# Sliding windows by DMA: thirteen staged batches instead of twelve, 32 KB packets on both queues, and a last store in three parts

## The chip, the core and the metric

The kernel runs on one core of one Trainium2 chip. The time is the device time of one execution, in microseconds; a smaller one is better. The program uses no compute engine. It consists of DMAs, which SP (SyncE) and ACT (ScalarE) issue, each on a queue of its own, and which the core's 16 DMA engines carry out. A DMA is cut into packets, and each engine works on the packets of both queues. A semaphore counts the engines that have finished a DMA: it rises by 16 for a whole one, and SP and ACT can wait for its value.

## The reference

The input is a float32 array of 32 batches, 4096 rows and 256 columns. Windows of 64 rows are taken every 32 rows, 127 in each batch, and written out one after the other:

```python
n_windows = (length - window_size) // stride + 1
result = np.zeros((batch, n_windows, window_size, dim), dtype=np.float32)
for i in range(n_windows):
    start = i * stride
    result[:, i] = x[:, start:start + window_size].copy()
```

A batch is 128 blocks of 32 rows, 32 KB each. Window w is blocks w and w + 1, 64 KB. Every block but the first and the last of a batch is thus written twice: as the first half of window w and as the second half of window w - 1. The output has 266.3 MB, the input 134.2 MB.

## The kernel before, in words

There are two ways to make a batch.

*Copied batches* go from HBM to HBM, issued by SP (`copy`, line 93). For a group of windows one DMA reads 64 KB for each window, at steps of 32 KB, and writes 64 KB for each. A copied batch is 8.3 MB through the DMA engines; HBM reads 8.3 MB and writes 8.3 MB. Before, a batch is three DMAs (`COPY_PARTS`, line 16): 80 windows in packets of 16 KB, 32 windows in packets of 32 KB, 15 windows in packets of 16 KB.

*Staged batches* go through on-chip memory, issued by ACT. `load` (line 75) brings the 128 blocks into a tile, one block of 32 KB per partition, 4.2 MB. `store` (line 83) writes the tile out twice: once with block p as the first half of window p, once with block p as the second half of window p - 1. That is 4.2 + 8.4 = 12.6 MB through the engines, but HBM reads only 4.2 MB. Before, the packets are 16 KB (`BLOCK_PARTS`, line 14). There are five tiles; the load of batch n waits for the stores of batch n - 5. ACT issues load 0 and load 1, and then in turn: wait for load n, two stores of n, load n + 2.

The stores of a staged batch have no gaps, and so each writes one half window too many: block 127 has no window 127, and lands in the first half window of the next batch; block 0 has no window -1, and lands in the last half window of the batch before. These *stray rows* must be overwritten. For most neighbours the order does it: the copy of a neighbour is issued by SP only after the staged batch has been stored (`after_store`, lines 134 to 137). These copies are called tied. Four neighbours, `EARLY`, are copied first of all, under a semaphore of their own; the staged batches beside them are stored only after that (line 146), and what they spoil is copied once more at the end by a *mend* of 32 KB, 16 packets of 2 KB (`half`, line 46; lines 151 to 158). Of the staged batches, numbered from n = 0, the last ones need mends.

Staged are the odd batches 1 to 23, twelve of them; copied are the other twenty. `_order` (line 102) lists the copies: the four early ones, then the untied ones, with each tied one inserted at a place that grows with the number of the last staged batch it waits for. SP issues all copies in this order, then waits for the early ones, issues the seven mends as their stores finish, waits for everything, and clears twelve semaphores one at a time (lines 159 to 163). The two queues are independent but for those semaphores, and they share the 16 engines.

Of the kernel before, what the change touches and what calls it, by code (L numbers as in the profile page):

```python
# [1 line left out]

# [4 lines left out]


STAGED = tuple(range(1, 24, 2))
BUFS = 5  # L10

EARLY = (18, 20, 22, 24)

BLOCK_PARTS = 2

COPY_PARTS = ((80, 4), (32, 2), (15, 4))


class _Geometry:


    def __init__(self, x, out, W, S):
        self.B, self.L, self.D = x.shape
        self.x, self.out = x, out
        self.n_win = (self.L - W) // S + 1
        self.n_blk = self.L // S
        self.blk = S * self.D
        self.win = W * self.D
        assert W == 2 * S and self.n_blk == self.n_win + 1 == 128

    def src(self, b, block, dims):

        at = (b * self.n_blk + block) * self.blk
        return bass.AP(self.x.tensor, self.x.offset + at, dims)

    def dst(self, b, half, dims):

        at = b * self.n_win * self.win + half * self.blk
        return bass.AP(self.out.tensor, self.out.offset + at, dims)

    def rows(self, b, w0, n):

        s, d = [[self.blk, n], [1, self.win]], [[self.win, n], [1, self.win]]
        return self.dst(b, 2 * w0, d), self.src(b, w0, s)

    def half(self, b, half, block):

        dims = [[self.blk // 16, 16], [1, self.blk // 16]]
        return self.dst(b, half, dims), self.src(b, block, dims)


class _Kernel:
    def __init__(self, nc, g, tiles):
        self.nc, self.g, self.tiles = nc, g, tiles
        self.loaded = [nc.alloc_semaphore(f"loaded{i}") for i in range(len(tiles))]
        self.stored = [nc.alloc_semaphore(f"stored{i}") for i in range(len(tiles))]
        self.copied = nc.alloc_semaphore("copied")
        self.early = nc.alloc_semaphore("early")
        self.count = {}

    def start(self, engine, out, in_, sem, parts=1):
        engine.dma_start(out=out, in_=in_, max_dma_last_dim=65536 // parts).then_inc(sem, 16)
        self.count[id(sem)] = self.count.get(id(sem), 0) + 16

    def all_of(self, engine, sem):
        engine.wait_ge(sem, self.count[id(sem)])

    def slot(self, n):
        return divmod(n, len(self.tiles))

    def after_store(self, engine, n):
        turn, i = self.slot(n)
        engine.wait_ge(self.stored[i], 32 * (turn + 1))

    def load(self, n):

        g, (_, i) = self.g, self.slot(n)
        if n >= len(self.tiles):
            self.after_store(self.nc.scalar, n - len(self.tiles))
        src = g.src(STAGED[n], 0, [[g.blk, g.n_blk], [1, g.blk]])  # L80
        self.start(self.nc.scalar, self.tiles[i][:, :], src, self.loaded[i], 2 * BLOCK_PARTS)

    def store(self, n):

        g, (turn, i) = self.g, self.slot(n)
        self.nc.scalar.wait_ge(self.loaded[i], 16 * (turn + 1))
        for half in (0, -1):
            dst = g.dst(STAGED[n], half, [[g.win, g.n_blk], [1, g.blk]])  # L90
            self.start(self.nc.scalar, dst, self.tiles[i][:, :], self.stored[i], 2 * BLOCK_PARTS)

    def copy(self, b, sem):

        w = 0
        for rows, parts in COPY_PARTS:
            self.start(self.nc.sync, *self.g.rows(b, w, rows), sem, parts)
            w += rows
        assert w == self.g.n_win


def _order(B):


    near = {b for s in STAGED for b in (s - 1, s + 1)}
    order = list(EARLY) + [b for b in range(B) if b not in near and b not in STAGED]
    tied = sorted(near - set(EARLY))
    n = len(order) + len(tied)
    for b in tied:
        behind = max(STAGED.index(s) for s in (b - 1, b + 1) if s in STAGED)  # L110
        order.insert(-(-(2 * behind + 5) * n // (2 * len(STAGED))), b)
    return order


@with_exitstack
def kernel(
    ctx: ExitStack,
    tc: tile.TileContext,
    x: bass.AP,
    window_size: bass.AP,  # L120
    stride: bass.AP,
    out: bass.AP,
):
    nc = tc.nc
    W, S = int(window_size), int(stride)
    g = _Geometry(x, out, W, S)
    assert 0 not in STAGED and g.B - 1 not in STAGED
    pool = ctx.enter_context(tc.tile_pool(name="blocks", bufs=1))
    tiles = [pool.tile([g.n_blk, g.blk], x.dtype, name=f"xb{i}") for i in range(BUFS)]

    with tc.tile_critical():
        k = _Kernel(nc, g, tiles)
        for b in _order(g.B):
            if b not in EARLY:
                for s in (b - 1, b + 1):
                    if s in STAGED:
                        k.after_store(nc.sync, STAGED.index(s))
            k.copy(b, k.early if b in EARLY else k.copied)
        k.load(0)
        waited = False  # L140
        last = len(STAGED) - 1
        for n, s in enumerate(STAGED):
            if n < last:
                k.load(n + 1)
            if not waited and (s - 1 in EARLY or s + 1 in EARLY):
                k.all_of(nc.scalar, k.early)
                waited = True
            k.store(n)


        k.all_of(nc.sync, k.early)
        for n, s in enumerate(STAGED):
            if s - 1 in EARLY or s + 1 in EARLY:
                k.after_store(nc.sync, n)
            if s - 1 in EARLY:
                k.start(nc.sync, *g.half(s - 1, 2 * g.n_win - 1, g.n_blk - 1), k.copied)
            if s + 1 in EARLY:
                k.start(nc.sync, *g.half(s + 1, 0, 0), k.copied)
        for n in range(len(STAGED)):
            k.after_store(nc.sync, n)  # L160
        k.all_of(nc.sync, k.copied)
        for sem in [*k.loaded, *k.stored, k.copied, k.early]:
            nc.sync.sem_clear(sem)


# [1 line left out]
_INS = ['x', 'window_size', 'stride']  # L167
_OUTS = [((32, 127, 64, 256), 'float32')]

_NUMBERS = {'window_size': 64, 'stride': 32}  # L170


# [26 lines left out]
```

## Time and profile before

| | us |
|---|---|
| median of three runs | 767.76 (767.14 to 767.97) |
| the profiled execution | 768.4 |
| its span, first to last instruction | 766.6 |
| mean rate of the DMA engines over the span | 414 GB/s |
| read from and written to HBM | 217.02 and 267.35 MB |

The page names two queues: q1 is SP's, q10 is ACT's. "DMA share" in a list of stretches is the mean share of time that the 16 engines spent on packets; records of neighbouring packets overlap slightly, so 1.01 can occur. The rate counts each byte once, also for a copy that reads and writes HBM. A line "SPq ... <- DMA ..." in the list of waits says how long SP waited in total for DMAs of that kind, how often, and the longest wait. The trace also has a record of every packet: queue, size, start and duration, without the engine.

The DMAs of the profiled execution, by kind, with the median time from issue to landing:

| DMA | number | KB each | us to landing |
|---|---|---|---|
| copy of 80 windows, SP | 20 | 5120 | 114.8 |
| copy of 32 windows, SP | 20 | 2048 | 116.7 |
| copy of 15 windows, SP | 20 | 960 | 97.7 |
| mend, SP | 7 | 32 | 48.3 |
| load, ACT | 12 | 4096 | 123.2 |
| store, ACT | 24 | 4096 | 84.6 |

### The profile page before, as it was taken

What the parts mean: (1) busy time and instruction counts of PE and PEld (TensorE: products, weight loads), DVE (VectorE), ACT (ScalarE), POOL (GpSimd) and SP (SyncE); (2) the same over time, 40 slices, a digit from 0 to 9 for tenths busy, and PEclk for the clock granted to TensorE, in tenths of its full rate; (3) what the DMA queues carried; (4) which work ended last, traced back from release to release, by engine and by line L of the source; (5) the groups of instructions that cost most, each with busy time, mean ns of one, the idle gap of its engine ahead of it and who ended that gap; (6) DMA issues with size and microseconds to landing.
All of it is one profiled execution on the core that took longest, in us unless ns stands there. A gap on an engine that the chain in (4) does not pass through costs nothing. (4 is left out here: it accounts for less than half of the span.)

```text
span 766.6 us, 180 instructions
## 1 busy us (share of the span) xinstructions
POOL 0.2 (0%) x4
## 2 busy tenths in 40 slices
POOL 0000000000000000000000000000000000000000
DMA  8999999999999999999999999999999999999996
GB/s 371 425 410 421 405 428 431 408 411 427 423 415 421 431 415 425 432 408 416 427 420 417 431 420 420 423 428 410 414 427 419 422 428 418 417 428 421 420 406 237
DMA packets 19837, 317.70 MB, mean 414 GB/s; under 512 B 1628, under 2 KB 1628, under 8 KB 1740
## 3 DMA queue, kind: packets, MB, share of 16 engines
q1 hardware_dynamic: 10044, 166.70, 51.9%
q10 hardware_dynamic: 9792, 151.00, 47.3%
q14 instruction: 1, 0.01, 0.0%
HBM read 217.02 MB, written 267.35 MB: 632 GB/s over the span
## 5 line engine op out<-in xcount | busy, mean ns | idle before, releaser
L180 POOL MEMSET const-bfloat16-1.0<- 128x1 bf16 x1 | 0.1, 102 | 0.0
L180 POOL MEMSET const-uint8-127<- 128x1 uint8 x1 | 0.1, 102 | 0.0
L180 POOL MEMSET const-float32-0.0<- 128x1 f32 x1 | 0.1, 99 | 0.2 <-issue 0.2
L180 POOL MEMSET const-float32-1.0<- 128x1 f32 x1 | 0.1, 99 | 0.0
## 6 DMA issues: line engine op xcount, KB each, us to landing
out_dram<-in_x_dram SPq DMA_DIRECT2D x20, 5120.0 KB, 114.8
out_dram<-xb ACTq DMA_DIRECT2D x24, 4096.0 KB, 84.6
xb<-in_x_dram ACTq DMA_DIRECT2D x12, 4096.0 KB, 123.2
out_dram<-in_x_dram SPq DMA_DIRECT2D x20, 2048.0 KB, 116.7
out_dram<-in_x_dram SPq DMA_DIRECT2D x20, 960.0 KB, 97.7
out_dram<-in_x_dram SPq DMA_DIRECT2D x7, 32.0 KB, 48.3
```

Source lines behind the costliest of these rows:

```text
L180: nc = _bacc.Bacc("TRN2", target_bir_lowering=False, num_devices=1)
```

## The change

- The staged batches are 1, 3, ... 25, thirteen, and nineteen are copied. The early ones are 20, 22, 24 and 26.
- Every large packet is 32 KB, on both queues (`start` has `parts=2` as its default, 65536 / 2).
- A copied batch is two DMAs instead of three: 112 windows (seven for each engine) and 15 windows.
- The last staged batch (25) is stored in three parts of its partitions, each with its two halves: 0 to 31, 96 to 127, then 32 to 95. The first two contain block 0 and block 127, and so all stray rows; their four DMAs count on a new semaphore, `fringe`. The last two mends wait for `fringe`; the mends of earlier staged batches wait for their stores as before.
- At the end SP waits for every semaphore, those of the loads too, and clears them all with one instruction over a range.

The order on ACT is otherwise the same: load n + 2 after the stores of n, five tiles. ACT's wait for the early copies stands ahead of the stores of n = 9 (batch 19), before it was n = 8 (batch 17).

```diff
-STAGED = tuple(range(1, 24, 2))
+STAGED = tuple(range(1, 26, 2))
-EARLY = (18, 20, 22, 24)
-BLOCK_PARTS = 2
-COPY_PARTS = ((80, 4), (32, 2), (15, 4))
+EARLY = (20, 22, 24, 26)
+EVEN = 112
+LAST = ((0, 32), (96, 32), (32, 64))
...
-    def start(self, engine, out, in_, sem, parts=1):
+    def start(self, engine, out, in_, sem, parts=2):
         engine.dma_start(out=out, in_=in_, max_dma_last_dim=65536 // parts).then_inc(sem, 16)
...
-        self.start(self.nc.scalar, self.tiles[i][:, :], src, self.loaded[i], 2 * BLOCK_PARTS)
+        self.start(self.nc.scalar, self.tiles[i][:, :], src, self.loaded[i])
...
-    def store(self, n):
+    def store(self, n, p0, rows, sem=None):
...
         for half in (0, -1):
-            dst = g.dst(STAGED[n], half, [[g.win, g.n_blk], [1, g.blk]])
-            self.start(self.nc.scalar, dst, self.tiles[i][:, :], self.stored[i], 2 * BLOCK_PARTS)
+            dst = g.dst(STAGED[n], 2 * p0 + half, [[g.win, rows], [1, g.blk]])
+            self.start(self.nc.scalar, dst, self.tiles[i][p0 : p0 + rows, :], sem or self.stored[i])
...
-        for rows, parts in COPY_PARTS:
-            self.start(self.nc.sync, *self.g.rows(b, w, rows), sem, parts)
-            w += rows
...
+        k.copy(b, 0, EVEN, k.early if early else k.copied)
+        k.copy(b, EVEN, n_win - EVEN, k.early if early else k.copied)
...
+        k.after_load(nc.scalar, n)
+        if n < last:
+            k.store(n, 0, g.n_blk)
+        else:
+            for p0, rows in LAST:
+                alone = p0 > 0 and p0 + rows < g.n_blk
+                k.store(n, p0, rows, None if alone else k.fringe)
...
+        if n == len(STAGED) - 1:
+            k.all_of(nc.sync, k.fringe)
+        elif s - 1 in EARLY or s + 1 in EARLY:
+            k.after_store(nc.sync, n)
...
-        for sem in [*k.loaded, *k.stored, k.copied, k.early]:
-            nc.sync.sem_clear(sem)
+def _end(k):
+    for sem in k.sems:
+        k.all_of(k.nc.sync, sem)
+    used = sorted(sem.num for sem in k.sems)
...
+    k.nc.sync.sem_clear(range(used[0], used[-1] + 1))
```

## The prediction

> **What bounds the kernel now.** I read the page's slices first, then its queue part, then stretches of the trace, then the waits, and last the packet records (queue, size, start, duration).
>
> ```profile
> span 766.6 us, 180 instructions
> DMA  8999999999999999999999999999999999999996
> DMA packets 19837, 317.70 MB, mean 414 GB/s; under 512 B 1628, under 2 KB 1628, under 8 KB 1740
> ...
> q1 hardware_dynamic: 10044, 166.70, 51.9%
> q10 hardware_dynamic: 9792, 151.00, 47.3%
> ...
> HBM read 217.02 MB, written 267.35 MB: 632 GB/s over the span
> ```
>
> No compute engine does anything; the 16 DMA engines are busy in every slice but the last. q1 is SP's queue (20 copied batches), q10 is ACT's (12 staged batches). Their shares add to 99.2% of 766.6, 760.5 us per engine. So every packet counts, and the time is the number of packets on an engine times the time of one, plus a start and an end.
>
> ```profile
> core 0: us, POOL busy (x), PEclk, DMA share, GB/s
> 6.00:26.00 20.00, 0.00 (x0) 1.00 1.01 432
> 657.00:670.00 13.00, 0.00 (x0) 1.00 1.00 408
> 720.00:748.00 28.00, 0.00 (x0) 1.00 0.94 403
> 752.00:756.00 4.00, 0.00 (x0) 1.00 0.92 348
> 756.00:758.00 2.00, 0.00 (x0) 1.00 0.78 286
> 758.00:760.00 2.00, 0.00 (x0) 1.00 0.74 246
> 760.00:762.00 2.00, 0.00 (x0) 1.00 0.29 110
> 762.00:764.00 2.00, 0.00 (x0) 1.00 0.06 22
> ```
>
> The last column is the rate. Clean stretches run at 432 GB/s, others lose some 5% with the engines still busy: there single packets take longer. From 720 the share is 0.94, as one engine of 16 has run out: the 15-row copies use 15 engines, so one has less to do. After 753 only copies are left (the last record of q10 ends at 753.4), and 15 engines move 348 instead of 403. That stretch and the engines' unequal ends, 758 to 764, are the tail.
>
> ```profile
> SPq L62 <- DMA out_dram<-xb: 61.2, 2, 40.2
> SPq L73 <- DMA out_dram<-xb: 19.2, 3, 9.4
> SPq L66 <- DMA out_dram<-in_x_dram: 7.7, 1, 7.7
> ```
>
> SP's waits for stores before mends and in the final list cost nothing while q1 holds queued copies. Only the last, 7.7 us for `copied`, sets the end: the last landing releases it at 764.9, twelve semaphore clears run from 764.9 to 765.6, and the closing barrier ends at 766.6.
>
> From the packet records: a 16 KB packet takes 611 ns undisturbed, a 32 KB one 1211. They overlap by a few ns; the next one on an engine starts 607.1 and 1209.4 ns after (432 GB/s over 16 engines also gives 607). Time over 611 and 1211, between 6 and 748 us: 16 KB of q1 1.87%, 32 KB of q1 3.16%, 16 KB of q10 2.70%; with start and tail 18.8 us per engine.
>
> **The account of before, for one of the 15 full engines.** A copied batch gives it 20 packets of 16 KB (80 rows), 4 of 32 KB (32 rows) and 4 of 16 KB (15 rows); a staged one 16 for the load and 32 for the two stores. In all 20 x 24 + 12 x 48 = 1056 of 16 KB and 80 of 32 KB: 1056 x 0.6071 + 80 x 1.2094 = 737.9 us. Plus 2.0 to the first packet, 18.8 of slow packets, and some 1.8 of mends and completion packets: 760.5, the mean end. The last engine ends 3.3 later, 763.8, its landing is seen at 764.9, the end at 766.6. The profiled execution took 768.4, 1.8 outside its span, and lies 0.6 above the median of 767.76; I add differences to the median.
>
> **The change, part by part.**
> *One more staged batch, and 32 KB packets.* A copied batch is now 16 packets of 32 KB on a full engine, a staged one 24: 19 x 16 + 13 x 24 = 616, times 1.2094 is 745.0 us. Against 737.9 that is **+7.1**: 8 packets more (+9.7), and 528 pairs of 16 KB packets turned into one each, 4.8 ns saved per pair (-2.5). The engines are never idle, so nothing hides it.
>
> *Slow packets.* No row has 32 KB on both queues. Slow packets go with copies: while the 80-row copies ran (equal packets on both queues) q1 lost 1.85% and q10 1.95%; while the 32-row copies ran (32 KB beside 16 KB, q1 taking 58% of engine time) they lost 3.0% and 5.65%. A copy reads and writes HBM, a staged packet does one of the two, so the larger share of copies asks more of HBM; alone the copies made 348 GB/s, 696 read and written. After the change packets are equal throughout. For q1 I take 1.85% of 304 x 1.2094 = 367.7: 6.8 us. For q10 the nearest is its whole run, as its loads and second stores lose most whatever copy lies beside them: 2.70% of 377.3, 10.2. With 0.6 at the start 17.6: **-1.2**. Ends: 0.96% (stretches of 4 us with a q1 share of 47 to 53%) gives 7.2 us, -11.6; 3.9%, the mean beside the 32-row copies, gives 29.1, +10.3.
>
> *The tail.* q1 has 304 packets to send, q10 312; with the queues alternating and q1 starting 3.8 us late (first packet at 5.8, against 2.0; three packets) q10 ends last with some 5 packets, 6 us of stores without copies. So the copies-only stretch goes (2.72 MB between 752 and 764 at 403 would be 6.7 us; it took until 763.8), but unequal ends, grown over the whole run, stay. Ends: 0 and -3.3; I take **-1.0**, nearer to 0, as equal rates in the tail do not level engines that arrive 5 us apart.
>
> *Fringe first.* The last batch's stores go out as partitions 0-31, 96-127, then 32-95: six DMAs for two, the same packets. Each of the four added costs ACT some 0.4 to 0.5 us of issue (median store 442 ns), covered by queued packets; at an empty queue it would be 2 us. SP's two last mends wait for the fringe instead of the whole store, with 8 packets per engine (9.7 us) still to come behind it. A mend issued at 756.2 had landed by 764.9 in a crowded queue, so they end about when the middle does: 0, and +3 if the middle is through first. Each fringe DMA has two partitions per engine; the nearest rows are ordinary stores: at their 2.7%, 0.3 us on 8 packets, inside the 10.2. Ends: 0, and +10 if each of the 8 takes twice as long (the slowest q10 packet took 1766 ns, 2.9 times 611).
>
> [...]
>
> *The end.* One ranged clear replaces twelve, of 57 ns each: **-0.6**. The longer list of waits passes at once but for its last few entries, 65 ns each (+0.1).
>
> *The order on SP and ACT.* EARLY moves by two, the wait for `early` from the store of n = 8 to n = 9; those copies land by 160 us, hundreds earlier. Tied copies wait for stores on SP. At 216 GB/s for each queue (half of 432) a copied batch takes 38.5 us and a staged one 58.3. The tightest is batch 18, the eighteenth copied, due on the engines at 5.8 + 17 x 38.5 = 660; the store it waits for (n = 9, after ten loads and stores and one load more) lands near 2 + 16.8 MB / 216 GB/s + 9 x 58.3 = 605. So SP's queue does not run dry: 0. SP issues 38 copies rather than 60, each behind a full queue: 0. If a wait did starve q1, q10 would keep the engines busy and the copies would trail alone, at 348 instead of 403: 1.3 us for each 10 us of lag.
>
> Sum: 7.1 - 1.2 - 1.0 + 0 - 0.6 + 0.1 = **+4.4** on 767.76: 772.2. I say **772**.
>
> **The rivals.**
> *Faster: equal packets empty the waits for HBM.* For it: beside equal shares 4 us stretches lost only 0.96%, and HBM bytes fall from 484 to 480 MB while DMA bytes rise. Against it: part of the slow packets are q10's own at the turn from store to load, and their count rises. Price: 2.0 + 745.0 + 7.2 + 1.6 + about 2.5 to the last engine, 1.0 + 1.2 to the end: 760.5, a time of 761.6. It decides below 13 us of slow packets. Chance 0.34.
>
> *Slower still: the fringe or 32 KB packets are expensive.* 3.9% slow, or a fringe at double time: +10 on the sum, 778 to 784. For it: 32 KB packets lost 3.16%, the most of any kind. Against: the 16 KB ones beside them lost 5.65%. Chance 0.16.
>
> *The tail does not do what it says:* q1 loses six turns, its copies end last, and the mends wait behind them: tail saving gone, +1 to +3: 773 to 775. Chance 0.08.
>
> **How the numbers follow.** My forecast, 768 to 776, has 0.42. Less than 0.2% (1.5 us) is no change to this measurement. Faster takes the first rival, 0.34; same the lower edge of the forecast, 0.10; slower the rest, 0.56. The range goes from 760, the faster case, to 780, inside the expensive one, leaving 0.2 out.
>
> **What the profile will show.** 321.8 MB, 158.4 of it on q1 and 163.6 on q10; 1209 ns between undisturbed 32 KB packets. Slow packets near 17 us: 7 or 29 picks a rival. The 0.94 share some 45 us from the end; q10 the last queue with data, at 420 GB/s or more after q1 is dry; fringe packets no slower than other stores; a single clear. I am wrong if slow packets do not follow the share of copies, if the fringe doubles, or if q1 ends last.

## The result

| | before | changed |
|---|---|---|
| median of seven runs, us | 767.51 (765.99 to 769.03) | 773.32 (771.89 to 779.07) |
| ratio | | 1.0092, 95% interval 1.0074 to 1.0110 |

The changed kernel is 0.9% slower, 5.8 us, where the prediction said 4.4 and 772. Five of its seven executions lie between 771.9 and 773.5; the other two took 777.1 and 779.1. The profiled execution is the one of 779.1, and its trace shows something that is not in the sum: one engine that came late. Its page:

```profile
span 776.9 us, 155 instructions
...
DMA  9999999999999999999999999999999999999993
...
DMA packets 11319, 321.95 MB, mean 414 GB/s; under 512 B 1389, under 2 KB 1389, under 8 KB 1501
...
q10 hardware_dynamic: 5680, 163.58, 50.0%
q1 hardware_dynamic: 5639, 158.37, 48.3%
HBM read 212.89 MB, written 267.42 MB: 618 GB/s over the span
```

The mean rate, 414 GB/s, is that of before; there are 4.25 MB more to move, though HBM has 4.1 MB less to read and write. The stretches at the end, in the columns busy share and GB/s:

```profile
core 0: us, POOL busy (x), PEclk, DMA share, GB/s
6.00:700.00 694.00, 0.00 (x0) 1.00 1.00 424
738.00:750.00 12.00, 0.00 (x0) 1.00 0.93 394
752.00:756.00 4.00, 0.00 (x0) 1.00 0.92 343
756.00:760.00 4.00, 0.00 (x0) 1.00 0.96 400
760.00:764.00 4.00, 0.00 (x0) 1.00 0.67 271
764.00:768.00 4.00, 0.00 (x0) 1.00 0.23 89
768.00:772.00 4.00, 0.00 (x0) 1.00 0.07 29
772.00:776.00 4.00, 0.00 (x0) 1.00 0.04 18
```

From 738 the engine without the 15-row work is idle (a share of 0.93, 15 of 16), as before the change from 720 (0.94); it is called the sixteenth engine below. From 768 to 775 a share of 0.07, one of 16, is busy: a single engine sends 32 KB packets of q10 one after the other, at 1213 ns each, until 774.7. The packet records, strung together by their starts and ends, show where it lost its time: five of its q10 packets between 706 and 727 took 1.6 to 2.9 us instead of 1.21, and one at 753.7 took 2.97, 7.4 us too much together.

The five belong to the stores of batch 23, which are whole. The semaphore of these stores, which rises once for each engine, rises for the last time at 740.3 and for the last but one at 735.0; for the load ahead of them the two are 0.3 apart. In the same time the sixteenth engine, with no copies left, was in the split store already: its eight fringe packets ran from 704.8 to 727.1, 1.2 to 4.1 us each, 22.2 us together.

The waits of SP:

```profile
SPq L83 <- DMA out_dram<-xb: 507.6, 9, 61.6
SPq L68 <- DMA out_dram<-xb: 216.9, 4, 74.6
SPq L72 <- DMA out_dram<-xb: 8.2, 1, 8.2
...
SPq L72 <- DMA out_dram<-in_x_dram: 0.2, 1, 0.2
```

The last long wait, 8.2 us, is now for a store and not for copies and mends, as the prediction had it: q10 ends last. A mend behind that store on the late engine adds 0.2. The instruction records have a single clear, at 775.8.

### The profile page after: what moved, and what is told of

Same layout as the page of the kernel before. It is cut to its first block, busy times and chain, and to the rows that moved or that the text cites. A ratio compares the mean times of both kernels' runs of the same rounds, so it can differ in the third digit from the quotient of the medians.

```text
span 776.9 us, 155 instructions
## 1 busy us (share of the span) xinstructions
POOL 0.2 (0%) x4
```

## The experiments

Each kernel is the changed one but for the edit shown. Times are medians; the kernel before ran beside them, 767.2 to 768.0 us. Two more kernels, which leave parts of the work out, ran once each and stand further down.

| kernel | us | ratio to before, 95% interval |
|---|---|---|
| changed | 773.3 | 1.0092 (1.0074 to 1.0110) |
| last store whole | 772.0 | 1.0064 (1.0051 to 1.0077) |
| all packets 16 KB | 770.8 | 1.0056 (1.0038 to 1.0074) |
| 16 KB and last store whole | 772.6 | 1.0066 (1.0054 to 1.0078) |
| 12 staged, 32 KB | 770.5 | 1.0043 (1.0028 to 1.0058) |
| 10 staged, mixed sizes | 771.0 | 1.0048 (1.0033 to 1.0062) |
| 12 staged, 48 windows in 32 KB | 772.8 | 1.0066 (1.0052 to 1.0080) |
| 12 staged, finer turns | 771.1 | 1.0053 (1.0037 to 1.0068) |
| 12 staged, middle windows by batch | 785.4 | 1.0241 (1.0220 to 1.0262) |
| 12 staged, 32 and 48 windows | 768.0 | 1.0011 (1.0002 to 1.0020) |
| every store split | 799.8, 815.7 (two executions) | |

"Slow packets" below are, as in the prediction, the time of all packets beyond 611 and 1211 ns, per engine. Where they are given for a kernel, they come from its one profiled execution.

### The last store whole

```diff
-LAST = ((0, 32), (96, 32), (32, 64))
+LAST = ((0, 128),)
```

> The changed kernel with its last staged batch stored whole, two DMAs of 128 partitions; the last two mends wait for all of it. My theory (the split is worth little, the slowdown is the 8 more packets per engine): the mends are issued after the last store instead of beside its middle part, so the end comes 1 to 3 us later than in the changed kernel, about 774 to 776. Rival (the parts of 32 partitions cost several us): 765 to 769, as before the change.

771.97, and all six executions between 771.4 and 772.6. Slow packets come to 16.2 us, against 18.6 in the profiled execution of the changed kernel. The end looks different:

```profile
core 0: us, POOL busy (x), PEclk, DMA share, GB/s
752.00:756.00 4.00, 0.00 (x0) 1.00 0.96 414
756.00:760.00 4.00, 0.00 (x0) 1.00 0.91 390
760.00:764.00 4.00, 0.00 (x0) 1.00 0.43 181
764.00:768.00 4.00, 0.00 (x0) 1.00 0.07 22
768.00:772.00 4.00, 0.00 (x0) 1.00 0.03 9
```

The last 32 KB packet ends at 765.5, no engine trails by itself; the two mends, issued after it, land by 768.6, so the wait that the split removes is worth 3 us. Both theories missed: the split neither saved 1 to 3 us nor cost 4 to 8. It gave back about what it saved, and more in the two long executions of seven.

### All packets 16 KB, with the split and without

```diff
-    def start(self, engine, out, in_, sem, parts=2):
+    def start(self, engine, out, in_, sem, parts=4):
```

> The changed kernel with every large packet 16 KB instead of 32 KB, on both queues; 13 batches staged. My theory: 1232 packets at 607.1 ns are 747.9 us on a full engine against 745.0, and slow packets stay near 17 us, as the queues still alternate with equal packets: 3 us more than the changed kernel, 775 to 777. Rival (32 KB packets are what made it slower): at or below 768.

770.81, less than with 32 KB and not more. By count 16 KB costs 2.9 us; slow packets fell from 18.6, the late engine's among them, to 13.9. The rival is not right either: 13 batches stay 3.6 us above before. And with the last store whole as well:

> The changed kernel with both its packet size and its last store undone: 13 staged batches, all packets 16 KB, the last store whole, one ranged clear. It leaves the thirteenth batch alone as the difference. My theory: floor 747.9 us against 737.9 before, slow packets near 14 as with 16 KB and the split: 769 to 772, close to the kernel that had 16 KB and the split (770.8), since the split neither gives nor takes in most executions. Rival (the split helps by letting mends land beside the middle part): 773 to 774.

772.61, 4.6 above the kernel before. That isn't the thirteenth batch alone: the copies also are two DMAs instead of three, without the 32 KB packets that 32 windows had before, and 12 staged batches with 16 KB packets throughout were not run. Each taken against the kernel before that ran beside it, the split gave 1.0 us here (3.6 against 4.6) and cost 1.0 with 32 KB (5.8 against 4.8); in both pairs the intervals of the ratios overlap. In the profile of this kernel the last 16 KB packet ends at 767.4 and the mends land at 770.4: the 3 us again. So the split does two things, it saves up to 3 us of mends and pays with slow packets, and neither sign of the net is shown.

### 12 staged batches, 32 KB packets

```diff
-STAGED = tuple(range(1, 26, 2))
+STAGED = tuple(range(1, 24, 2))
-EARLY = (20, 22, 24, 26)
+EARLY = (18, 20, 22, 24)
```

> The changed kernel with 12 staged batches, as before the change, and all packets 32 KB. My theory: 608 packets are 735.3 us on a full engine against 745.0, but SP's queue has 320 packets against 288, so that some 29 packets of copies trail alone at 348 instead of 403 GB/s, 41 us for what would take 35: 9.7 less, 5.5 more, and the mends behind them: 768 to 770. Rival (the size of the packets made it slower, not the thirteenth batch): 773 or more, with slow packets above 17 us before the copies are alone.

770.46, a little above the expected range. ACT's queue sent its last packet at 715.5, and copies were alone until 764.5:

```profile
core 0: us, POOL busy (x), PEclk, DMA share, GB/s
6.00:700.00 694.00, 0.00 (x0) 1.00 1.00 425
716.00:758.00 42.00, 0.00 (x0) 1.00 0.93 324
758.00:762.00 4.00, 0.00 (x0) 1.00 0.55 222
```

The mechanism is as expected, and the rate of copies alone, 324 GB/s on 15 engines, is lower than the 348 that the tail of before had shown; that stretch still had 1.4 us of stores in it. So with equal packets 12 is too few for the queues to end together, and 13 costs 9.7 us of packets. Before the change SP's queue moved 52% of the large packets' bytes up to 700, here 50%; with the larger share, which it had there with mixed sizes in three DMAs, 12 were nearly enough.

### Copies alone

The staged batches, the mends and the waits for stores are gone; nineteen copied batches remain.

```diff
-        for n in [] if early else _beside(b):
-            k.after_store(nc.sync, n)
...
-        _staged(k)
-        _mends(k)
```

> Left out: everything staged; only the nineteen copied batches, with no waits. It measures the rate of copies by themselves. My theory (copies ask HBM for two bytes per byte moved, and HBM is the limit): 325 to 350 GB/s as in the tails, 158 MB in 455 to 490 us, packets near 1.5 us. Rival (the slow packets have nothing to do with HBM's total): 405 to 432 GB/s, 370 to 390 us.

488.3 us (one execution).

```profile
DMA packets 5415, 158.14 MB, mean 325 GB/s; under 512 B 589, under 2 KB 589, under 8 KB 589
...
HBM read 158.14 MB, written 158.14 MB: 650 GB/s over the span
```

A 32 KB packet takes 1.58 us on average, against 1.24 in the changed kernel, where q10 has equal packets beside it. Here all 16 engines are busy (97.9% of the span), and they move no more than the 15 of the run before did in its copies-only stretch, 325 against 324 GB/s: so the number of engines is not the limit. Since each byte counts twice in HBM, this speaks for HBM, at some 650 GB/s, as the limit of copies; that is inferred, and the run shows neither the limit by itself nor which part of HBM it would be. The kernel before moves 632 GB/s of reads and writes over its span, close to it, and this is where its slow packets can come from.

### Stores in parts, alone and beside copies

Alone: the copies are left out but for two of 15 windows, and each of the thirteen batches is stored in the three parts, one batch after the other.

```diff
...
+        for p0, rows in LAST:
+            alone = p0 > 0 and p0 + rows < g.n_blk
+            k.store(n, p0, rows, None if alone else k.fringe)
         if n < last:
-            k.store(n, 0, g.n_blk)
-        else:
-            for p0, rows in LAST:
-                alone = p0 > 0 and p0 + rows < g.n_blk
-                k.store(n, p0, rows, None if alone else k.fringe)
+            k.all_of(nc.scalar, k.fringe)
```

> Left out: all copied batches (SP sends two DMAs of 15 windows and the mends). The thirteen staged batches remain, and each is stored in the three parts of partitions, 0-31, 96-127 and 32-95, one batch after the other. It shows the packets of a part of 32 partitions by themselves. [...] Theory B (the split is free): all packets near 1.21 us, a batch near 30 us, the whole near 400.

515.4 us (one execution), 39.6 for a batch: not the 30 of theory B. Stretches inside parts of 32 partitions (71 to 79, 112 to 118) and between them, in loads and parts of 64 (94 to 100, 133 to 139):

```profile
core 0: us, POOL busy (x), PEclk, DMA share, GB/s
71.00:79.00 8.00, 0.00 (x0) 1.00 1.04 225
94.00:100.00 6.00, 0.00 (x0) 1.00 0.99 421
112.00:118.00 6.00, 0.00 (x0) 1.00 1.07 229
133.00:139.00 6.00, 0.00 (x0) 1.00 1.01 431
```

The same engines at the same busy share move half as much; the median packet took 2.55 us in the first and the third stretch, 1.215 in the others. Beside the copies:

```diff
-        engine.wait_ge(self.stored[i], 32 * (turn + 1))
+        engine.wait_ge(self.stored[i], 96 * (turn + 1))
...
         if n < last:
-            k.store(n, 0, g.n_blk)
+            for p0, rows in LAST:
+                k.store(n, p0, rows)
```

> The changed kernel with every staged batch stored in the three parts, not only the last; copies beside them as before. Theory A (the small parts cost engine time also beside copies): 3 to 8 us for each of the twelve more, 810 to 870 in all. Theory B (free beside copies, as these use the engine half of the time): 772 to 778.

799.8 us in the profiled execution (a second took 815.7): 26 more than the changed kernel for twelve more splits, 2.2 each, under theory A's least and far from B.

```profile
core 0: us, POOL busy (x), PEclk, DMA share, GB/s
6.00:700.00 694.00, 0.00 (x0) 1.00 1.00 422
740.00:756.00 16.00, 0.00 (x0) 1.00 0.95 309
756.00:772.00 16.00, 0.00 (x0) 1.00 0.91 281
```

Up to 700 the rate is nearly that of the changed kernel, 424: beside copies the parts hardly slow the engines. But q10 falls behind, copies end at 730.8, and what is left of q10 goes on alone at 281 to 309 GB/s until 795.9. So the price of the split depends on whether copies lie beside it. The changed kernel shows the same: of the 80 packets of q10 that start between 735 and 750, nearly all of them fringe, none took over 1222 ns; of the 129 from 750 to 764, as the copies run out, twelve took 1.5 to 3.2 us, and the stretch from 752 to 756 has 343 GB/s.

### 10 staged batches

```diff
-STAGED = tuple(range(1, 26, 2))
+STAGED = tuple(range(1, 20, 2))
-EARLY = (20, 22, 24, 26)
+EARLY = (14, 16, 18, 20)
-EVEN = 112
+COPY_PARTS = ((48, 4), (64, 2), (15, 2))
...
-        self.start(self.nc.scalar, self.tiles[i][:, :], src, self.loaded[i])
+        self.start(self.nc.scalar, self.tiles[i][:, :], src, self.loaded[i], 4)
```

> The other way: 10 staged batches in 16 KB packets, 22 copied ones with 48 windows in 16 KB and 79 in 32 KB packets, so that both queues send about as many packets (484 and 480 on a full engine) and end together; the ending is that of the changed kernel. A staged batch costs an engine 8 packets of 32 KB more than a copied one. My theory: floor 480 + 12 x 22 packets of 16 KB and 5 x 22 of 32 KB, (480 + 264) x 0.6071 + 110 x 1.2094 = 584.7 us is not the count: 10 staged at 48 and 22 copied at 12 of 16 KB and 5 of 32 KB give 744 and 110, 451.7 + 133.0 = 584.7, too low by the windows of the 15-row DMA counted once, so I go by bytes: 10 x 24 + 22 x 16 = 592 packets of 32 KB, 716 us. With slow packets at 3.9 to 4.5% (28 to 32 us, as beside the 32-row copies before): 716 + 30 + 8 = 754, 750 to 760. Rival (HBM is full at this share of copies, slow packets take back what the count gives): 766 or more.

(The count in its middle is wrong: a copied batch has 10 packets of 32 KB on a full engine here, not 5; 744 x 0.6071 + 220 x 1.2094 = 717.8 us agrees with the 716 by bytes.) 771.0, the rival. The count fell by 20 us; slow packets rose from 19 to 41.6, most of all on the 32 KB copies (6.7% up to 725, 5.6% on ACT's queue). ACT's queue was through at 725.7 and copies trailed alone.

```profile
core 0: us, POOL busy (x), PEclk, DMA share, GB/s
6.00:700.00 694.00, 0.00 (x0) 1.00 1.01 411
726.00:758.00 32.00, 0.00 (x0) 1.00 0.95 331
...
HBM read 225.28 MB, written 267.22 MB: 640 GB/s over the span
```

The 640 GB/s lie near the 650 of copies alone. Fewer staged batches give the engines less to do (20 us by count) and HBM more (492.5 MB read and written against 484.4), and slow packets took back what the count gave.

### Attempts at a better version of 12

All have 12 staged batches, 16 KB packets on ACT's queue, the last store whole and the ranged clear. They differ in the copies' sizes and turns.

```diff
+COPY_PARTS = ((64, 4), (48, 2), (15, 4))
```

> 12 staged batches in 16 KB packets; copies of 64 windows in 16 KB, 48 in 32 KB and 15 in 16 KB packets, so that SP's queue gets a little more of each engine than before the change and ends with ACT's; the last store whole, one ranged clear. My theory: the floor is that of before, 737.9 us; the copies-alone tail of 10 us at 348 GB/s shrinks, the clears save 0.6, slow packets stay near 19: 763 to 767. Rival (a larger share of copies brings as many slow packets as the tail gives back): 767 to 769.

772.8: it overshot. SP's queue ended at 750.2, ACT's at 767.1, with slow packets at 23.1. Worse than the rival expected: there are 4 us more of slow packets than before, and the mends come after the trailing stores.

```diff
+COPY_PARTS = ((32, 4), (16, 2), (32, 4), (16, 2), (16, 4), (15, 4))
```

> 12 staged batches in 16 KB packets and the copies' sizes of before (96 windows... 80 and 15 in 16 KB, 32 in 32 KB), but in finer turns: 32 windows in 16 KB, 16 in 32 KB, 32 in 16 KB, 16 in 32 KB, 16 and 15 in 16 KB. The last store whole, one ranged clear. My theory (slow packets come where the copies' share is high for some microseconds): shorter stretches of 32 KB packets bring fewer slow ones, 13 to 17 us instead of 19: 762 to 766. Rival (the mean share decides): 766 to 768.

771.1: neither theory. Slow packets were fewer while both queues ran (12.7 us from 6 to 708, before the change 17.6), but SP's queue moved 50% of the large packets' bytes up to 700 instead of 52, ACT's ended at 716.3, and copies trailed alone:

```profile
core 0: us, POOL busy (x), PEclk, DMA share, GB/s
6.00:706.00 700.00, 0.00 (x0) 1.00 1.01 424
720.00:756.00 36.00, 0.00 (x0) 1.00 0.94 326
```

Why the same packets in shorter DMAs, with 16 and 32 KB in finer alternation, get fewer turns stays open.

```diff
+COPY_PARTS = ((0, 80, 4), (80, 32, 2), (112, 15, 4))
+EVEN_PARTS = ((0, 64, 4), (79, 32, 2), (111, 16, 4))
...
+    def middle(self, w0):
...
+        dst = g.dst(0, 2 * w0, _middle_dims(g.n_win * g.win, g.win))
+        src = g.src(0, w0, _middle_dims(g.n_blk * g.blk, g.win))
+        self.start(self.nc.sync, dst, src, self.copied, 4)
...
```

`_middle_dims` makes sixteen windows, each two batches from the one before.

> 12 staged batches, sizes as before, but the 15 windows that a batch leaves over after 112 are, for the sixteen even batches, windows 64 to 78, and one DMA copies one such window of all sixteen batches, so that all 16 engines get one each; only the four odd copied batches still use 15 engines. The last store whole, one ranged clear. My theory: the sixteenth engine no longer runs out 40 us early; a full engine has one window (2.4 us) less: 763 to 766. Rival (16 engines that read 8 MB apart get in each other's way in HBM): these DMAs run slower, 768 or more.

785.4, the rival. The sixteenth engine did stay busy (a share of 1.01 and 433 GB/s from 720 to 732), but slow packets rose to 37.6 us, and the mean rate to 700 was 411.

```profile
core 0: us, POOL busy (x), PEclk, DMA share, GB/s
6.00:700.00 694.00, 0.00 (x0) 1.00 1.01 411
720.00:732.00 12.00, 0.00 (x0) 1.00 1.01 433
```

The reads of the new DMAs are 8 MiB apart, which no other kernel here has. That the distance is the reason was not tested by itself.

```diff
+COPY_PARTS = ((80, 4), (32, 2), (15, 4))
+COPY_MORE = ((64, 4), (48, 2), (15, 4))
...
+        for rows, parts in COPY_MORE if b % 3 == 0 else COPY_PARTS:
```

> 12 staged batches in 16 KB packets; the copies of before (32 windows in 32 KB packets) in thirteen batches, and 48 windows in 32 KB packets in the other seven, those whose number is divisible by three; the last store whole, one ranged clear. Before the change the copies trailed alone for 10 us, with 48 windows in every batch ACT's queue trailed for 17. My theory: seven of twenty batches bring the ends within a few us of each other, slow packets come to about 19, the clears save 0.6: 764 to 767. Rival (each larger share of copies costs as much as it gives back): 768 to 771.

768.0 against 767.6, 0.1% more, and at the lower edge of the rival's range. The queues did end together, at 760.1 and 761.3, and the end of the span came 0.7 us earlier in the profiled executions (765.9 against 766.6), but that is less than executions differ; slow packets were 18.9. No version beat the kernel before.

## Why the prediction was right, and where it was not

*One more staged batch and 32 KB packets, +7.1.* Right. The mean of all packets at their undisturbed spacing, over 16 engines, is 734.8 us before and 742.1 after, +7.3; the spacing of 32 KB packets in the changed kernel is 1209 to 1210 ns, as taken. The engines' busy share up to 700 is 1.00, so nothing hides it.

The median execution, 773.3, has no trace: the 1.4 us between the sum and the measurement can't be divided among the terms, and that the sum came so near is in part luck, since in the one execution that has a trace the tail was 6 us longer than before and not 1 shorter.

*Slow packets, -1.2.* The sum was nearly right: 17.6 taken, 18.6 measured in the profiled execution and 16.2 with the last store whole, against 19.0 before. Its parts were off in opposite directions: between 6 and 748 us q1 lost 2.4% for 1.85 taken, q10 2.3% for 2.70. That their number follows the share of copies is borne out by 10 staged batches (41.6 us) and by copies alone (1.58 us per packet). That size plays a part was not expected: 13.2 us with 16 KB and 16.2 with 32, both with the last store whole. The larger packets save 2.9 by count, and the two kernels take the same time (ratios 1.0066 and 1.0064). The rival of nearly empty waits, 761.6, was half right: with equal packets and 13 batches slow packets were fewer, 13.2 us with 16 KB and the store whole against 19.0 before, but not 7.

*The tail, -1.0.* Right for a whole last store, wrong for the changed kernel. q10 did end last (q1's last 32 KB packet at 763.0, q10's at 774.7). Strung together, the last of the 15 full engines ended 4.0 us after their mean before the change, 3.3 with the last store whole and 3.0 with 16 KB packets as well: 0.6 to 1.0 less, as taken, though there the mends follow 3 us behind. With the split it was 4.2 in the profiled execution with 16 KB, and 10.1 in that of the changed kernel, 7.6 us behind the next engine (its last 32 KB packet ended at 774.7, the next engine's at 767.1). The prediction also wanted 420 GB/s there; 15 engines at 1209.4 ns a packet come to 406, and with the store whole the stretches from 752 to 760 have 414 and 390. One reading of its account of before was off: 760.5 us is busy time, over 16 engines and with the overlap of the records in it, and not the mean end of a full engine, which is 759.2. Of the sum only the tail's far end, -3.3, rests on it; by 759.2 it is -4.0.

*Fringe first, 0.* Wrong, by one of the prediction's own signs: fringe packets were slower than other packets where no copies lay beside them, 2.55 us at the median in the run without copies against 1.215. The prediction kept +10 as an upper end; the nearest row, an ordinary store, was the wrong neighbour. By themselves the parts of 32 partitions run at 225 to 229 GB/s against 421 to 431 in the stretches between them. In the run with all stores split, where copies lay beside them until 730.8, a split cost 2.2 us. Against it stand 3 us of mends that no longer follow the last store. The net, +1.0 with 32 KB and -1.0 with 16 KB, is within the noise.

The late engine fits the fringe as well. The sixteenth engine took 22.2 us for its eight fringe packets, where with the last store whole it sent eight packets of the same store in 12. In both profiled kernels with the split one engine fell behind in the whole stores of batch 23, while the sixteenth engine was in its fringe packets: the last engine was done with these stores 5.3 us after the last but one with 32 KB and 2.8 with 16 KB, against 0.5 and 1.2 in the two with the last store whole. What ties the two engines together, if anything does, is not shown: the records don't tell which partitions a packet reads, and of the two long executions only one has a trace. The eleven executions with the store whole had no such case; with 16 KB and the split two of six, the profiled one among them, lie 2 us above the others. Slow early q10 packets on an engine that has run out of copies are also in the trace of before (690 to 706, 16 KB packets at 1.1 to 1.2 us), so that another cause exists, which no run explains.

*The end, -0.6 + 0.1.* Right: one clear at 775.8, and the landing that releases it is seen at 775.3 and 775.7; from the last one to the end of the span 1.2 us, before 1.8.

*The rivals.* "More expensive", +10 on the sum, came near in two of seven executions (777.1 and 779.1), and the fringe that it named is the likeliest reason, within the limits just told. "The tail doesn't do what it says", with q1 last, did not occur with 13 and occurred with 12 (copies alone for 48 us).

## What to carry to other kernels

When all engines are busy to the end, count packets per engine first: that gave +7.1 here where +5.8 was measured, and everything else came to a few microseconds either way in the median. Then ask what else the packets share: with 10 staged batches the count fell by 20 us and the time rose by 3.8, with 41.6 us of slow packets instead of 19.0. Two queues that share the engines should end together, and their shares moved here with the sizes of packets and of DMAs (SP's queue had 52% of the large packets' bytes up to 700 before, 50% with 32 KB throughout and 50% with the sizes of before in shorter DMAs); measure where each queue ends before changing the amount of work on one. A last transfer that is cut to let something else start sooner should keep all the partitions in each piece, or be run by itself once: parts of 32 of the 128 partitions ran at 225 to 229 GB/s by themselves, and the stretches between them at 421 to 431.

## What the runs showed of the hardware that was not expected

- HBM to HBM copies alone make 325 GB/s, 650 GB/s of reads and writes, with packets of 1.58 us instead of 1.21; 15 engines make the same (324). Mixed with as many staged packets all 16 make 424.
- 16 KB packets lose less than 32 KB ones in the same kernel: 13.2 against 16.2 us with the last store whole, about the 2.9 us that larger packets save by count.
- A queue's share depends on more than the sizes of its packets: the same sizes in the same amounts, in six DMAs and finer alternation instead of three, let ACT's queue end at 716 instead of 753.
- Stores of 32 partitions run at half the rate by themselves (225 to 229 GB/s against 421 to 431), but cost the engines almost nothing in total while copies run beside them (422 against 424 GB/s; none of 80 packets over 1222 ns in the changed kernel); the price falls due when the copies end (281 to 309 GB/s with every store split), and on an engine that ran out of copies early (22.2 us for eight fringe packets, where eight of the whole store took 12).
